# A decoder block on one core: convolution taps shared with ScalarE, attention dealt over weight tiles, merge products with tokens on the partition

## The chip, the cores and the metric

The kernel runs on one core of one Trainium2 chip. The metric is device time in microseconds (us) of one execution; the time before is 1765.85 us, the median of three runs (1764.63 to 1767.06). The engines are named as the profile names them: PE (TensorE matmul), PEld (its weight load), DVE (VectorE), ACT (ScalarE), POOL (GpSimd) and SP (SyncE, which issues most transfers).

## What is computed

One layer of a hybrid decoder for 256 tokens of width 2048, batch 1, all in float32:

```python
ada = silu(c) @ w_ada + b_ada                       # six vectors of 2048: shift, scale, gate, twice
h = rmsnorm(x) * (1 + sc1) + sh1
proj = h @ w_in                                      # 11824 columns: q, 6 x K/V, branch gates, GLU, merge gates
o_nsa = nsa_attention(q, k/v compressed, selected, window, gates)   # 16 heads of 128, 2 groups
y_a = o_nsa @ w_o_nsa
u = causal_dwconv(a * sigmoid(g), w_dw, b_dw)        # 31 taps per channel
y_b = silu(layernorm(u)) @ conv_pw_w + conv_pw_b
merged = sigmoid(ga) * y_a + sigmoid(gb) * y_b
x = x + g1 * (merged @ w_out)
h = rmsnorm(x) * (1 + sc2) + sh2
x = x + g2 * conv_ffn(h)                             # 2048 -> 2 x 5632 -> 2048
out = rmsnorm(x)
```

With 256 tokens every block is selected, and the window covers all earlier tokens, so that the selected and the window branch are two causal attentions over all keys.

## The kernel before

All weights, about 400 MB, are read once. A weight tile is 128 rows by 1024 numbers (for a product 512 columns wide: two of its sixteen blocks of 128 rows). `wtile` loads it into `raw` through SP's queue, ACT casts it to a rounded part `hi` (L213), and DVE subtracts to get the rest, `lo` (L214). Activations are split alike. A product is three matmuls per block, hi by hi, hi by lo and lo by hi, summed in PSUM. `raw` has four buffers; `hi` and `lo` have three in the pool `wp`, and between `more.__enter__()` (L467) and `more.__exit__` (L735) each fourth tile uses one more buffer out of a pool of its own.

There are three forms of product. `prod_x` (L228) has the activations as stationary operand and 512 weight columns moving; its result has tokens on the partition. `prod_w` (L240) has 128 weight columns as stationary operand and the 256 tokens moving; its result has channels on the partition. `prod_p` (L254) serves the up-projection of the last stage. Two result buffers of PSUM (`acc`) are shared by all of them.

The products follow each other: GLU columns (channel blocks 0 to 6 with the adaLN sums, then blocks 7 to 15), K/V, four chunks of queries (`q_chunk`), three of the four merge gates `gate_a`, four products with `w_o_nsa` (the fourth gate ahead of the last), four gates `C_MB`, four products with `conv_pw_w`, five with `w_out`, then the channel-mixing part. A `w_o_nsa` product takes the heads in their order: its tile number i needs heads 2i and 2i+1.

Other work is cut into steps in three queues: `heads_q` (attention), `conv_q` (convolution and its LayerNorm), `ada_q` (adaLN sums on DVE, each step a transfer of 512 KB into one of two `araw` buffers and one instruction, L280). After each weight tile `tick` (L117) gives out steps as long as the planned load of their engines is not above PE's. `drain` gives out what is left of a queue. The order on each engine is then set by a scheduler that models the time of each instruction; steps of `heads_q` get a higher priority. On the chip each engine runs its list in that order.

A step `scores(h)` makes the scores of one head for both branches, adds the distances (L684), takes the maximum (L686) and the exponential (L688); `values(h)` scales the rows (L704), transposes them (L709 to L711), copies them out of PSUM (L713), multiplies with the values (L714, L715) and splits the result into `oT`, the operand of the `w_o_nsa` products. `compressed(g)` does the compressed branch of a group of eight heads.

The convolution takes two channel blocks at a time (`conv_blocks`, L443): ACT makes the first product with the bias (L450), DVE adds 30 taps per block in place, one instruction of 128 by some 240 each (L457), and ACT copies the sum back (L460). The LayerNorm follows in steps once all blocks are done.

The merge keeps channels on the partition: `merged` gets `y_a` times its gate (L831), `gbs` the other gates (L840), and after each `conv_pw_w` product four instructions add the bias and multiply (L851), two add (L853) and the sums are split into `mT` (L854), the stationary operand of the `w_out` products.

## Time and profile before

| | |
|---|---|
| median of three runs | 1765.85 us |
| the profiled execution | 1765.94 us |
| its span, first to last instruction | 1764.2 us |
| PE busy | 1712.7 us, 97% |
| PEld busy | 1551.8 us, 88% |
| DVE busy | 1286.4 us, 73% |
| ACT busy | 872.9 us, 49% |
| mean granted PE clock | 0.986 of full speed |
| transfers | 402.8 MB read, 230 GB/s over the span |

Matmuls are pipelined and their ends are modelled, so that a busy PE need not run at its best rate; how fast it runs is seen from the distance between the starts of matmuls that follow each other. From 178 us on the products of the list above follow without a break: the second GLU products start there, the first `q_chunk` at 363, the first `gate_a` at 489, the first `w_o_nsa` product at 596, the first `C_MB` gate at 714, the first `conv_pw_w` product at 812, `w_out` at 907 and the channel-mixing part at 1012 us.

### The profile page before, as it was taken

How to read it: one execution, taken by the hardware profiler on the slowest of the kernel's cores; microseconds unless marked ns; L12 is line 12 of the kernel's file. 1: busy time of each engine (PE TensorE's matmuls, PEld its weight loads, DVE VectorE, ACT ScalarE, POOL GpSimd, SP SyncE). 2: the span in 40 equal slices, each digit the busy share in tenths (PEclk: the TensorE clock that was granted, in tenths of full speed). 3: DMA queues.
4: the chain of work that ended last, by engine and by line, in shares of the span. 5: the costliest groups of instructions: out<-in, count | busy, mean ns of one | idle time of the engine just before them, and what ended most of it. 6: DMA issues, size and time to landing. Idle time of an engine off the chain costs nothing.

```text
span 1764.2 us, 29690 instructions
## 1 busy us (share of the span) xinstructions
PE 1712.7 (97%) x11844; PEld 1551.8 (88%) x11844; DVE 1286.4 (73%) x1852; ACT 872.9 (49%) x1223; POOL 5.5 (0%) x22
## 2 busy tenths in 40 slices
PE   5999999999999999999999899999999999999997
PEld 3777999899999999999988888888888888888886
DVE  2233999998999898877886677776467776586665
ACT  4333444344768634563344465554455554345553
POOL 0000000000000000000000000000000000000000
PEclk8999999999999999999999999999999999999999
DMA  9996777884764676789887667676666767656663
GB/s 305 352 345 225 228 225 231 266 286 143 235 198 130 203 241 214 250 300 317 292 306 259 199 202 226 215 224 222 219 213 212 220 213 219 212 183 189 188 192 127
DMA packets 270198, 406.83 MB, mean 231 GB/s; under 512 B 12876, under 2 KB 181612, under 8 KB 269420
## 3 DMA queue, kind: packets, MB, share of 16 engines
q1 hardware_dynamic: 268652, 400.49, 71.4%
q10 hardware_dynamic: 1408, 4.46, 0.7%
q8 instruction: 92, 1.51, 0.4%
q14 instruction: 46, 0.38, 0.1%
HBM read 402.80 MB, written 2.10 MB: 230 GB/s over the span
## 4 chain that ended last, share of the span: by engine, by line
PE 93%; DMA 3%; DVE 2%; ACT 1%; issue 1%; SPq 0%; DVEq 0%; ACTq 0%
PE accp L261 18%; PE accw L251 11%; PE accw L248 11%; PE accw L250 11%; PE accp L262 9%; PE accx L236 6%; PE accx L237 6%; PE accx L235 6%; DMA araw<-in_w_ada_dram 2%; PE pt L379 1%; PE pt L675 1%; DVE lo L214 1%; PE pt L714 1%; PE pt L409 1%; PE pt L410 1%; PE pt L411 1%
## 5 line engine op out<-in xcount | busy, mean ns | idle before, releaser
L213 ACT CAST hi<-raw 128x1024 fp32r<-128x1024 f32 (+2 forms) x562 | 575.1, 1024 | 765.9 <-PE accw L250 273.3
L214 DVE TENSOR_TENSOR lo<-raw,hi 128x1024 fp32r<-128x1024 f32 (+2 forms) x562 | 668.6, 1191 | 375.4 <-ACT hi L213 363.8
L261 PE MATMUL accp<-act,hi 128*128 128x512 f32 x1408 | 492.4, 395 | 0.0
L251 PE MATMUL accw<-act,lo 128*128 128x256 f32 x1696 | 484.1, 286 | 2.0 <-DVE lo L214 2.0
L250 PE MATMUL accw<-act,hi 128*128 128x256 f32 x1696 | 483.8, 285 | 0.0
L248 PE MATMUL accw<-act,hi 128*128 128x256 f32 x1696 | 483.8, 285 | 0.0
L262 PE MATMUL accp<-act,lo 128*128 128x256 f32 x1408 | 393.6, 280 | 0.0
L251 PEld LDWEIGHTS accw<-act,lo 128*128 128x128 f32 x1696 | 325.5, 192 | 5.0 <-DVE lo L214 3.0
L248 PEld LDWEIGHTS accw<-act,hi 128*128 128x128 f32 x1696 | 325.8, 192 | 3.2 <-issue 2.4
L250 PEld LDWEIGHTS accw<-act,hi 128*128 128x128 f32 x1696 | 325.7, 192 | 2.4 <-issue 2.2
L261 PEld LDWEIGHTS accp<-act,hi 128*128 128x128 f32 x1408 | 264.1, 188 | 62.1 <-issue 0.2
L262 PEld LDWEIGHTS accp<-act,lo 128*128 128x128 f32 x1408 | 265.6, 189 | 0.3 <-issue 0.2
L236 PE MATMUL accx<-lo,act 128*128 128x512 f32 (+2 forms) x664 | 227.6, 343 | 1.3 <-DVE lo L214 1.3
L235 PE MATMUL accx<-hi,act 128*128 128x512 f32 (+2 forms) x664 | 227.2, 342 | 0.0
L237 PE MATMUL accx<-hi,act 128*128 128x512 f32 (+2 forms) x664 | 226.8, 342 | 0.0
L457 DVE SCALAR_TENSOR_TENSOR cacc<-big,cw,cacc 128x255 f32<-128x255 f32 (+24 forms) x480 | 201.3, 464 | 0.3
L280 DVE SCALAR_TENSOR_TENSOR t<-araw,cs,t 128x1024 f32<-128x1024 f32 x120 | 153.6, 1280 | 25.3 <-DMA araw<-in_w_ada_dram 25.2
L236 PEld LDWEIGHTS accx<-lo,act 128*128 128x128 f32 x664 | 125.8, 189 | 18.4 <-DVE lo L214 2.6
L235 PEld LDWEIGHTS accx<-hi,act 128*128 128x128 f32 x664 | 125.8, 189 | 14.5 <-ACT hi L213 0.2
L237 PEld LDWEIGHTS accx<-hi,act 128*128 128x128 f32 x664 | 125.8, 189 | 14.3 <-issue 0.4
L918 DVE SCALAR_TENSOR_TENSOR t<-t,fw,t 128x254 f32<-128x254 f32 (+1 forms) x176 | 73.5, 478 | 0.0
L916 ACT ACTIVATE t<-t,fw 128x256 f32<-128x256 f32 x88 | 48.0, 593 | 1.3 <-DVE t L913 1.3
(214 smaller groups left out, 1198.7 us busy)
## 6 DMA issues: line engine op xcount, KB each, us to landing
araw<-in_w_ada_dram SPq DMA_DIRECT2D x192, 512.0 KB, 5.4
raw<-in_ffn_w_up_dram SPq DMA_DIRECT2D x176, 512.0 KB, 4.5
raw<-in_w_in_dram SPq DMA_DIRECT2D x116, 512.0 KB, 4.6
raw<-in_ffn_w_down_dram SPq DMA_DIRECT2D x88, 512.0 KB, 4.7
raw<-in_w_in_dram SPq DMA_DIRECT2D x48, 384.0 KB, 3.9
raw<-in_w_o_nsa_dram SPq DMA_DIRECT2D x32, 512.0 KB, 4.7
raw<-in_conv_pw_w_dram SPq DMA_DIRECT2D x32, 512.0 KB, 5.5
raw<-in_w_out_dram SPq DMA_DIRECT2D x32, 512.0 KB, 4.7
```

The lines of the kernel that those rows point to most:

```text
L213: nc.scalar.copy(hi[:, :n], raw[:, :n])
L214: los.append(nc.vector.tensor_tensor(lo[:, :n], raw[:, :n], hi[:, :n], op=ALU.subtract).ins)
L235: nc.tensor.matmul(o, act[:, k, 0, s], hi, start=k == 0, stop=False)
L236: nc.tensor.matmul(o, act[:, k, 0, s], lo, start=False, stop=False)
L237: nc.tensor.matmul(o, act[:, k, 1, s], hi, start=False, stop=k == nk - 1)
L248: nc.tensor.matmul(acc[:, b, :], hi[:, s], act[:, k, 0, :], start=k == 0 and b % 2 == 0, stop=False, skip_group_check=True)
L250: nc.tensor.matmul(acc[:, b, :], hi[:, s], act[:, k, 1, :], start=False, stop=False, skip_group_check=True)
L251: nc.tensor.matmul(acc[:, b, :], lo[:, s], act[:, k, 0, :], start=False, stop=last, skip_group_check=True)
L261: nc.tensor.matmul(acc[:, b], hi[:, s], act[:, k], start=k == 0, stop=False, skip_group_check=True)
L262: nc.tensor.matmul(acc[:, b, 0, :], lo[:, s], act[:, k, 0, :], start=False, stop=k == KB - 1, skip_group_check=True)
L280: nc.vector.scalar_tensor_tensor(acc, raw, cs[:, k:k + 1], acc, op0=ALU.mult, op1=ALU.add)
L457: nc.vector.scalar_tensor_tensor(acc[:, s:], u[:, b, :T - s], cw[:, CW - 1 - s, b:b + 1], acc[:, s:], op0=ALU.mult, op1=ALU.add)
```

## The change

The convolution takes three blocks at a time into one wide tile `cacc`. For 18 of the 31 taps (`WIDE`) ACT makes three products, one per block, into `cprod`, and DVE adds all three with one instruction of 128 by some 720 (`wide`); 12 taps stay as they were, and the first product too. `cacc` and `cprod` have one buffer each; the last addition writes back to `u`, so that the copy L460 goes. The pool with the extra `hi` and `lo` buffers goes.

Steps of `heads_q` are no longer given out by planned load but at an even rate per weight tile, which `deal(n)` sets: the steps then in the queue over n tiles. `AHEAD` falls from 2 to 1: scores run one head ahead of values, and the score tiles have two buffers in place of three. `PACE`, the planned cost of the transfer of an adaLN step, rises from 5000 to 6500, and planned PE time from 2.53 to 2.75 per column. The adaLN steps for `g1` enter their queue when the convolution and the LayerNorm steps queued by then have been given out (`conv_done`) and not at the end of the attention.

Sixteen products (four each of `gate_a`, `w_o_nsa`, `C_MB`, `conv_pw_w`) go from `prod_w` to `prod_x`. The merge has tokens on the partition, with the bias loaded as a row for all partitions; `merged` is turned back by 32 transposes on PE (`turn_m`), given out three and four tiles after their product through the list `coming`.

```diff
-AHEAD = 2
+AHEAD = 1
-PACE = 5000
+PACE = 6500
...
+    def deal(n):
+        share[:] = len(heads_q) / n, 0.0
...
     def tick():
+        for c in coming:
+            c[0] -= 1
+        while coming and coming[0][0] <= 0:
+            coming.popleft()[1]()
+        share[1] += share[0]
+        while heads_q and share[1] >= 1.0:
+            share[1] -= 1.0
+            give(heads_q)
...
-            for q in queues:
+            for q in (conv_q, ada_q):
...
-        pool, bufs = (ext[0], 1) if ext[0] is not None and turn[0] % 4 == 0 else (wp, 3)
-        hi = pool.tile([P, WT], F32R, tag="hi", name=nm("hi"), bufs=bufs)
-        lo = pool.tile([P, WT], F32R, tag="lo", name=nm("lo"), bufs=bufs)
+        hi = wp.tile([P, WT], F32R, tag="hi", name=nm("hi"))
+        lo = wp.tile([P, WT], F32R, tag="lo", name=nm("lo"))
...
+    WIDE = tuple(s for s in range(2, CW) if s % 5 not in (0, 2)) + (1,)
...
+        def product(b, s):
+            def f():
+                if b == b0:
+                    box["p"] = cvp.tile([P, n, T], F32, tag="cprod", name=nm("cprod"))
...
+                nc.scalar.mul(box["p"][:, b - b0, s:], u[:, b, :T - s], cw[:, CW - 1 - s, b:b + 1])
+            return f
+
+        def wide(s):
+            def f():
+                acc, prod = box["a"], box["p"]
+                if s == 1:
+                    nc.vector.tensor_add(u[:, b0:b0 + n, :], acc, prod)
+                else:
+                    nc.vector.tensor_add(acc[:, :, s:], acc[:, :, s:], prod[:, :, s:])
+            return f
...
+        narrow = deque(({"dve": 470}, tap(b, s)) for s in range(2, CW) if s not in WIDE for b in blk)
+        for s in WIDE:
+            conv_q.extend(({"act": 500}, product(b, s)) for b in blk)
+            conv_q.extend(narrow.popleft() for _ in range(min(n, len(narrow))))
+            conv_q.append(({"dve": 170 + n * 265}, wide(s)))
...
-        gp = prod_w(h1, w_in, C_MA + n * 512, 512)
-        sg = sgt([P, 4, T])
+        gp = prod_x(h1, w_in, C_MA + n * 512, 512)
+        sg = sgt([P, NT, 512])
...
         heads_q.extend(compressed(0) + heads(0, HG))
+        deal(18)
         q_chunk(2)
         q_chunk(3)
         heads_q.extend(compressed(1) + heads(HG, HG))
+        deal(23)
         sga = [gate_a(n) for n in range(3)]
...
-        yp = prod_w(oT, w_o_nsa, n * 512, 512)
-        nc.vector.tensor_mul(merged[:, 4 * n:4 * n + 4, :], yp, sg)
+        yp = prod_x(oT, w_o_nsa, n * 512, 512)
+        nc.vector.tensor_mul(merged[:, :, n * 512:(n + 1) * 512], yp, sg)
...
+    def turn_m(b):
+
+        def f():
+            p_ = pt([P, 2, T])
+            for j in range(2):
+                for t in range(NT):
+                    nc.tensor.transpose(p_[:, j, t * P:(t + 1) * P], merged[:, t, (b + j) * P:(b + j + 1) * P], ident)
+            split(mT[:, b:b + 2], p_)
...
+        yp = prod_x(uT, conv_pw_w, n * 512, 512)
+        y = t4([P, NT, 512])
+        for t in range(NT):
+            nc.vector.tensor_add(y[:, t, :], yp[:, t, :], bias)
+            nc.vector.tensor_mul(y[:, t, :], y[:, t, :], gbs[:, t, s])
+            nc.vector.tensor_add(merged[:, t, s], merged[:, t, s], y[:, t, :])
+        coming.extend([3 + i, turn_m(4 * n + 2 * i)] for i in range(2))
```

Three places show how the order on the engines moves. The first is PE where the second group of eight heads meets the first `w_o_nsa` product. Before, that product (written accw, with `act` as the operand `oT`) has started while transposes (L709 to L711) and value products (L714, L715) of late heads of the group stand between its matmuls:

```order
L251 MATMUL accw_6514<-act_189,lo_6753 128x256
L248 MATMUL accw_6794<-act_4536,hi_6796 128x256
...
L248 MATMUL accw_6794<-act_4536,hi_6796 128x256
L709 MATMUL pt_6175<-ident,s_6036 128x128
L714 MATMUL pt_6144<-t_884_6150,big_3234 128x256
L710 MATMUL pt_6175<-ident,s_6041 128x128
L715 MATMUL pt_6144<-t_884_6150,big_3234 128x128
```

Now, in the same place, the first four of that product's eight tiles stand ahead, and behind them the group begins: the transposes of the compressed part (L699), the scores of its first heads (L718) and their values (L749 to L758), with no matmul of a product between.

```order
L250 MATMUL accx_6727<-hi_6800,act_4680 128x512
L699 MATMUL pt_5930<-ident,t_865_5909 128x128 x4
L718 MATMUL pt_5965<-big_3302,big_4008 128x2x128
L718 MATMUL pt_5967<-big_3302,big_4008 128x512
...
L749 MATMUL pt_6055<-big_3302 128x256
L752 MATMUL pt_6057<-ident,s_5971 128x128
...
L753 MATMUL pt_6160<-ident,s_6019 128x128
...
L248 MATMUL accx_6727<-hi_6825,act_4680 128x512
```

All eight heads of the second group have moved behind the first half of the first `w_o_nsa` product, into its second half and the product after it.

The second place is ACT in the middle of a group of heads. Before, what stands between the exponentials (L688), scalings (L704) and copies (L713) of the heads are casts of weight tiles (L213) and a few instructions of the convolution:

```order
L688 ACTIVATE s_5756,st_5750<-s_5756,st_5749 128x256 x2
L713 COPY t_809_5805<-pt_5801 128x384
L704 ACTIVATE s_5697<-s_5697,st_5708 128x128 x2
L704 ACTIVATE s_5702<-s_5702,st_5708 128x256 x2
L713 COPY t_811_5813<-pt_5809 128x384
L213 CAST hi_6550<-raw_6549 128x1024
L460 COPY big_190<-cacc_5452 128x256
L460 COPY big_190<-cacc_5454 128x256
L213 CAST hi_6583<-raw_6582 128x1024
```

Now, at the start of the second group, products of the last three convolution blocks (L495) stand between the exponentials (L731) and scalings (L747), three for each tap:

```order
L226 CAST hi_6874<-raw_6873 128x1024
L701 COPY big_3302<-pt_5930 128x512
L495 ACTIVATE cprod_6469<-big_190,cw 128x245 x3
L731 ACT_TABLE_LOAD
L731 ACTIVATE s_5971,st_5970<-s_5971,st_5969 128x128 x2
L731 ACTIVATE s_5976,st_5970<-s_5976,st_5969 128x256 x2
L495 ACTIVATE cprod_6560<-big_190,cw 128x243 x3
L731 ACTIVATE s_6014,st_6013<-s_6014,st_6012 128x128 x2
L731 ACTIVATE s_6019,st_6013<-s_6019,st_6012 128x256 x2
L747 ACTIVATE s_5971<-s_5971,st_5982 128x128 x2
L747 ACTIVATE s_5976<-s_5976,st_5982 128x256 x2
L495 ACTIVATE cprod_6661<-big_190,cw 128x242 x3
```

From the copy L701 to the last head's split stand 39 such products, eight heads and seven casts of weight tiles on ACT.

The third place is PE in the fourth `conv_pw_w` product. Before, only its matmuls stand there; now the transposes of the columns that the third one finished (L903) are set among them, a first one early and three later, for two pairs of blocks:

```order
L248 MATMUL accx_8868<-hi_8940,act_7681 128x512
L903 MATMUL pt_8929<-ident,big_6725 128x128
L903 MATMUL pt_8957<-ident,big_6725 128x128
L249 MATMUL accx_8868<-lo_8941,act_7681 128x512
...
L248 MATMUL accx_8868<-hi_8971,act_7681 128x512
L903 MATMUL pt_8929<-ident,big_6725 128x128 x3
L903 MATMUL pt_8957<-ident,big_6725 128x128 x3
L249 MATMUL accx_8868<-lo_8972,act_7681 128x512
```

The turned columns of the last product stand in the same way inside the first `w_out` product.

## Rows read from the trace of the kernel before

**Rows 1.** The page: busy time of engines; the chain that ended last, by engine.

```profile
PE 1712.7 (97%) x11844; PEld 1551.8 (88%) x11844; DVE 1286.4 (73%) x1852; ACT 872.9 (49%) x1223; POOL 5.5 (0%) x22
...
PE 93%; DMA 3%; DVE 2%; ACT 1%; issue 1%; SPq 0%; DVEq 0%; ACTq 0%
```

**Rows 2.** PE in order of time: start us, duration, instruction; inside a prod_w product.

```profile
459.14 0.28 PE L248 MATMUL accw<-act,hi 128*128 128x256 f32 x1
459.26 0.28 PE L250 MATMUL accw<-act,hi 128*128 128x256 f32 x1
```

**Rows 3.** The same, inside a prod_x product 512 columns wide.

```profile
960.18 0.39 PE L237 MATMUL accx<-hi,act 128*128 128x512 f32 x1
960.41 0.39 PE L235 MATMUL accx<-hi,act 128*128 128x512 f32 x1
960.64 0.39 PE L236 MATMUL accx<-lo,act 128*128 128x512 f32 x1
```

**Rows 4.** Stretches: length, busy (instructions) by engine, PE clock, DMA; one product each.

```profile
789.30:812.30 23.00, 23.00 (x194) 23.00 (x193) 16.49 (x14) 9.30 (x9) 0.00 (x0) 1.00 0.92 304
...
957.70:979.40 21.70, 21.70 (x97) 18.00 (x96) 12.20 (x12) 9.78 (x12) 0.00 (x0) 1.00 0.69 221
```

**Rows 5.** PE in order of time: two transposes that follow each other.

```profile
463.22 0.27 PE L709 MATMUL pt<-ident,s 128*128 128x128 f32 x1
463.33 0.27 PE L710 MATMUL pt<-ident,s 128*128 128x128 f32 x1
```

**Rows 6.** Stretches with attention, all instructions.

```profile
413.60:595.60 182.00, 182.00 (x1340) 171.22 (x1339) 165.35 (x361) 124.67 (x294) 0.52 (x1) 0.98 0.55 165
595.60:624.30 28.70, 28.70 (x233) 28.18 (x232) 25.06 (x39) 15.37 (x23) 0.00 (x0) 1.00 0.82 274
```

**Rows 7.** The first of them, only what writes or reads the tile accw.

```profile
413.60:595.60 182.00, 133.38 (x962) 121.57 (x961) 0.00 (x0) 5.07 (x5) 0.98 0.55 165
```

**Rows 8.** Groups by line: busy us, mean ns, idle before; ACT's work for the heads.

```profile
L688 ACT ACTIVATE s<-s,st 128x128 f32<-128x128 f32 (+1 forms) x64 | 28.5, 447 | 1.4 <-DVE st L686 1.1
...
L704 ACT ACTIVATE s<-s,st 128x128 f32<-128x128 f32 (+1 forms) x64 | 23.8, 446 | 1.1 <-DVE st L694 1.1
...
L713 ACT COPY t<-pt 128x384 f32<-128x384 f32 x32 | 14.6, 473 | 9.1 <-PE pt L711 8.9
...
L688 ACT ACTIVATION_READ_ACCUMULATOR s<-s,st 128x1 f32 x64 | 12.1, 189 | 0.0
...
L329 ACT CAST act<-pt 128x256 fp32r<-128x256 f32 x16 | 5.9, 370 | 12.5 <-PE pt L715 12.4
```

**Rows 9.** Groups by line and shape, ACT: casts of weights, a scaling, a first product.

```profile
L213 ACT CAST hi<-raw 128x1024 fp32r<-128x1024 f32 x476 | 499.9, 1051 | 639.2 <-PE accw L250 225.8 <-PE accx L237 169.3 <-PE accp L261 154.8
...
L704 ACT ACTIVATE s<-s,st 128x256 f32<-128x256 f32 x32 | 14.3, 497 | 0.0
...
L450 ACT ACTIVATE cacc<-big,par,cw 128x256 f32<-128x256 f32 x16 | 9.3, 598 | 0.5 <-DVE big L436 0.4
```

**Rows 10.** Groups by line, DVE: taps, and a product of 128 by 768.

```profile
L457 DVE SCALAR_TENSOR_TENSOR cacc<-big,cw,cacc 128x255 f32<-128x255 f32 (+24 forms) x480 | 201.3, 464 | 0.3
...
L480 DVE TENSOR_TENSOR big<-accw,sg 128x768 f32<-128x768 f32 x3 | 2.9, 950 | 0.0
```

**Rows 11.** Stretches: GLU to second query chunk; a C_MB gate; two w_out products; their end.

```profile
177.90:413.60 235.70, 235.70 (x1983) 227.28 (x1982) 219.08 (x386) 102.57 (x127) 1.27 (x3) 1.00 0.81 245
...
737.70:766.30 28.60, 27.69 (x221) 26.53 (x220) 25.50 (x26) 24.01 (x32) 0.00 (x0) 1.00 0.75 249
...
907.40:957.70 50.30, 48.96 (x233) 40.26 (x232) 37.10 (x40) 21.56 (x25) 0.00 (x0) 1.00 0.85 286
...
1002.00:1012.30 10.30, 5.76 (x31) 5.47 (x29) 8.63 (x31) 6.07 (x15) 0.00 (x0) 0.70 0.80 262
```

**Rows 12.** The chain that ended last, 895 to 935 us: start us, us, what.

```profile
898.92 5.54 DMA araw<-in_w_ada_dram
...
905.86 5.42 DMA araw<-in_w_ada_dram
...
924.79 6.82 DMA araw<-in_w_ada_dram
```

144 lines of the change are left out of this document (73 added, 71 removed).

## The prediction

> **What bounds the kernel now.** I read first the page's busy shares and its chain. PE is busy 97% of the span, and 93% of the chain that ended last is PE [rows 1]: the time is the length of PE's stream plus the gaps in which something comes late. So an edit is priced by what it adds to or takes from that stream, and work on DVE, ACT or a queue costs only where PE then waits for it. Since a busy PE need not run at its best rate, I next read PE in order of time for the distance between starts [rows 2, 3, 5], and then stretches cut at the first matmul of each product, in which a product's own length stands beside what it took here [rows 4, 6, 7, 11]. The groups by line give the durations on ACT and DVE [rows 8 to 10]. The sum is made against the profiled execution, 1765.9 us (a span of 1764.2 and 1.7 around it), which is 0.1 above the median of the runs, so a result by it stands for the median too.
>
> **Sixteen products in another form.** A `prod_w` matmul of 256 columns starts 0.12 us after the one before it (459.14, 459.26) [rows 2]; a product has 192 of them, 23.0 us, and an undisturbed one took 23.00 [rows 4]. A `prod_x` matmul of 512 columns starts 0.23 us after its predecessor (960.18, 960.41, 960.64) [rows 3]; a product has 96, and an undisturbed one took 21.70 with 97 [rows 4]. So one wide matmul costs some 13 ns less than two narrow ones, 1.25 us per product (my value, between the 1.3 of the stretches and the 1.2 of the rounded starts), and the sixteen products get 20.0 us shorter. This term rests on a form that before uses already for `w_out`.
> The Trainium skill speaks against it: "TensorE: Matmul & The Clock Gate", section Back-to-back issue gap, gives as the isolated gap of warm matmuls the columns divided by 2.4 plus 2.5 ns, so that joining two saves 2.5 ns; for 1536 joined pairs that is an estimate of 3.8 us in place of 20. The trace does not agree: 0.12 and 0.23 us stand above the page's 0.109 and 0.216. The same section gives 131 ns for 512 columns in a stream of weight loads and matmuls, which no row here comes near.
>
> **The merge.** The `turn_m` steps add 32 transposes; two that follow each other start 0.11 us apart (463.22, 463.33) [rows 5], so 3.5 us; if none overlapped, 32 x 0.27 = 8.6. I take 3.5, since they stand in a stream of matmuls. They are given out three and four tiles after their product, and the last ones are needed by `w_out` only at tile 6 of 8, 16 us after that product began; DVE's merge (four instructions per 512 columns, and now six of 128x512 and a split) has that long: nothing on the path. The sigmoids are as many numbers as before.
>
> **Attention.** Before, 182 us with two query chunks and three gates hold 962 matmuls of accw [rows 6, 7], 962 x 0.12 = 115.4. The other 66.6 us, and the 28.7 - 23.0 = 5.7 by which the first `w_o_nsa` product is longer [rows 6], are 72.3 us for 16 heads and the compressed parts: 4.5 us of PE per head, waits included. ACT needs per head (28.5 + 12.1 + 23.8 + 14.6 + 5.9) / 16 = 5.3 us [rows 8].
> The first group now lies over two chunks and three gates: 2 x 23 + 3 x 21.8 = 111, with 8 x 4.5 = 36 makes 147 us of PE. ACT has there 8 x 5.3 = 42.5, some 40 casts at 1.051 [rows 9], some 81 products at 0.497 (a scaling of 128x256 [rows 9]) and copies of 6 us: 131. It fits, and with half the heads in that stretch some of the old waits go: -3 (between -6 and 0).
> The second group is not even. By the order it lies behind four tiles of the first `w_o_nsa` product, with 39 convolution products between its steps. From the copy L701 on ACT has 39 x 0.497 = 19.4, 8 x 5.3 = 42.5, seven casts 7.4 and some 2 for the copy and a table: 71 us. PE has 36 and ten tiles of 21.7 / 8 = 2.7: 63. PE cannot run ahead, since its next matmuls read what ACT's steps make: +8 at least. `cprod` and `cacc` have one buffer, so that in each of 13 steps ACT can wait for DVE's addition, about 0.95 us by the product of 128x768 [rows 10]: 0 to 13 more. I take +9, near the lower end, because the order puts exponentials and scalings between the products, which fill the time of an addition. Both groups: +6, from +2 to +21.
>
> **Convolution.** From the GLU to the second chunk DVE is busy 219.1 of 235.7 us and ACT 102.6, and PE loses little [rows 11]. Before, 242 of the 480 taps lie there at 201.3 / 480 = 0.42 [rows 10]: 101 us. Now, by the order, 108 taps (45 us), 40 additions of up to 768 columns (0.93, somewhat under the 0.95 of [rows 10]: 37) and 18 of one block (0.4: 7): 89. DVE gains 12 us in the stretch that it bounds next. ACT gets some 150 products at 0.497 (between 0.45 and the 0.598 of a first product [rows 8, 9]): 75 more, 178 of 234 us. What can be lost is the slack: the fourth `hi` and `lo` are gone, and DVE now waits for ACT's products, ahead of splits on its queue that PE needs. +1, from -1 to +6.
>
> **LayerNorm and adaLN steps.** The second `C_MB` product took 28.6 us for 23 [rows 11], beside the LayerNorm. The convolution now ends inside the second `w_o_nsa` product and the LayerNorm moves with it: 0, from -4 to +3. Two `w_out` products took 50.3 us [rows 11] for 2 x 21.7 and 1.8 of waiting work, some 5 lost while the chain waits for `araw` transfers of 5.4 to 6.8 us [rows 12]. By the order none of these steps stands in `w_out` now; 25 stand in the four `conv_pw_w` products, 31 in the five before. They read as many bytes, one transfer of 512 KB each beside a weight stream that already moves 304 GB/s [rows 4], so the loss may come back there. +1.5, from -8 to +8 with what a full queue of SP costs the weight tiles behind it.
>
> **Clock.** In the stretch of attention the granted clock was 0.98 on average [rows 6], and 0.70 around PE's wait for the adaLN sums at 1002 to 1012 [rows 11], that is, part of the time at the lower level of 1.2 GHz. 0.02 x 182 = 3.6 us is what the first one cost. A longer wait in the second group could bring one such stretch more: 0 in the sum, up to +7 in the range.
>
> **Sum.** 1765.9 - 20.0 + 3.5 + 6 + 1 + 0 + 1.5 = 1757.9, so 1758 us. What lies before 178 and after 1012 us stays.
>
> **The rivals.**
> A, cover everywhere: the attention costs +2, the waits of `w_out` and LayerNorm go (-5 and -3 in place of +1.5 and 0): 1757.9 - 4 - 6.5 - 3 = 1744, at 1741 to 1751. For it: no `araw` step in `w_out`, and the LayerNorm is spread. Against it: ACT's 71 us against PE's 63.
> E, the gain is half given back: attention at +12 with the `cprod` waits, or the convolution at +6: 1762 to 1769, near no change.
> B, ACT becomes the bound, and the result is slower: in the second group the `cprod` turns cost their full 13 us, attention is +21 less nothing from the first group, the clock falls once more (+3.6): 1765.9 - 20 + 3.5 + 21 + 3.6 + 1 + 1.5 = 1776.6, at 1770 to 1778. It decides once all losses together pass 16.5 + 3.5 = 20 us. For it: the order shows no product's matmul between the transposes and values of the second group, so nothing fills PE's waits. Against it: its scores run one head ahead.
> C, the change does not shorten PE's stream: if the columns alone set the distance of starts, a wide matmul takes 2 x 0.12 = 0.24 us, the first term is 0 and the sum 1777.9; with some of A's cover 1772 to 1778. The rows stand against it [rows 2 to 4], which show both forms at a granted clock of 1.00.
> By the Trainium skill's section Back-to-back issue gap (its 3.8 us in place of 20.0) the time would be an estimate of 1774, inside C.
> That the steps are not dealt evenly, as the change says, is seen in the order already and is in the sum.
>
> **Chances and range.** The forecast, 1752 to 1762, has 0.38; A 0.22, E 0.17, B 0.20, C 0.03. The likeliest gives the time, 1758. The range of 8 in 10 goes from 1743, which leaves out the lower end of A, to 1776, which takes in C and most of B: 1743 to 1776. A measurement of this kernel tells some 0.2% from no change, 3.5 us. Faster than 1762.3 are the forecast and A, 0.60; E lies within, 0.17; B and C are slower, 0.23.
>
> **What the profile after will show.** Starts of accx 0.23 us apart in gates and `conv_pw_w`, and undisturbed products of 21.7 us, show the first term right; 0.24 would make it wrong. The transposes of `turn_m` should start 0.11 us apart with no wait ahead. The first two `w_o_nsa` products should take together about 43.4 + 36 + 9 = 88 us with ACT busy nearly throughout and PE idle in front of transposes and values; 80 or less speaks for A, 100 and a granted clock under 1.00 for B. From 178 to 413 PE should lose no more than now, with DVE less busy and ACT near three quarters. `w_out` should have products of 21.7, and the `conv_pw_w` ones at most 2 us more than that each; if the chain waits for `araw` or for weight tiles there by more, the +1.5 is wrong. What would make the whole wrong is a place that I do not see in these rows: weight tiles late in the stretch of attention for want of the fourth buffer, or a cast behind a product that waits for DVE.

## The result: 1.5% slower

The changed kernel takes 1792.6 us (median of four runs, 1788.1 to 1795.0) against 1765.2 of the kernel before in the same comparison: a ratio of 1.0147, with a 95% interval of 1.0125 to 1.0170. The forecast was 1758 with a range of 1743 to 1776: wrong in its sign, and outside the range. The profiled execution, the longest of the four, took 1794.96 us, 29.0 more than that of before.

### The profile page after: what moved, and what is told of

Read it like the earlier page. It is cut to its first block, busy times and chain, and to the rows that moved or that the text cites. A ratio compares the mean times of both kernels' runs of the same rounds, so it can differ in the third digit from the quotient of the medians.

```text
span 1793.0 us, 26879 instructions
## 1 busy us (share of the span) xinstructions
PE 1711.8 (95%) x10340; PEld 1475.5 (82%) x10340; DVE 1266.2 (71%) x1672; ACT 981.5 (55%) x1497; POOL 6.1 (0%) x28
## 4 chain that ended last, share of the span: by engine, by line
PE 84%; DVE 6%; DMA 5%; ACT 3%; issue 2%; DVEq 0%; SPq 0%; ACTq 0%
PE accp L281 18%; PE accx L249 11%; PE accx L248 11%; PE accx L250 11%; PE accp L282 9%; PE accw L263 4%; PE accw L262 4%; PE accw L260 4%; DMA araw<-in_w_ada_dram 4%; DVE lo L227 2%; PE pt L399 1%; DVE t L300 1%; PE pt L718 1%; PE pt L429 1%; PE pt L430 1%
## 5 line engine op out<-in xcount | busy, mean ns | idle before, releaser
L249 PE MATMUL accx<-lo,act 128*128 128x512 f32 (+2 forms) x1176 | 434.0, 369 | 14.5 <-DVE lo L227 14.4
L248 PE MATMUL accx<-hi,act 128*128 128x512 f32 (+2 forms) x1176 | 429.8, 366 | 4.4 <-ACT hi L226 2.2
L250 PE MATMUL accx<-hi,act 128*128 128x512 f32 (+2 forms) x1176 | 430.1, 366 | 0.0
L249 PEld LDWEIGHTS accx<-lo,act 128*128 128x128 f32 x1176 | 223.1, 190 | 55.3 <-DVE lo L227 20.3
L248 PEld LDWEIGHTS accx<-hi,act 128*128 128x128 f32 x1176 | 222.9, 190 | 40.9 <-ACT hi L226 2.7
L250 PEld LDWEIGHTS accx<-hi,act 128*128 128x128 f32 x1176 | 223.3, 190 | 35.4 <-issue 2.3
L263 PE MATMUL accw<-act,lo 128*128 128x256 f32 x672 | 191.4, 286 | 0.4 <-DVE lo L227 0.4
L260 PE MATMUL accw<-act,hi 128*128 128x256 f32 x672 | 190.7, 284 | 0.0
L262 PE MATMUL accw<-act,hi 128*128 128x256 f32 x672 | 190.5, 284 | 0.0
L495 ACT ACTIVATE cprod<-big,cw 128x248 f32<-128x248 f32 (+17 forms) x288 | 123.7, 488 | 19.5 <-DVE cacc L504 17.5
L260 PEld LDWEIGHTS accw<-act,hi 128*128 128x128 f32 x672 | 128.8, 192 | 2.0 <-issue 2.0
L263 PEld LDWEIGHTS accw<-act,lo 128*128 128x128 f32 x672 | 128.6, 192 | 2.3 <-issue 1.7
L262 PEld LDWEIGHTS accw<-act,hi 128*128 128x128 f32 x672 | 128.8, 192 | 1.9 <-issue 1.9
L504 DVE TENSOR_TENSOR cacc<-cacc,cprod 128x756 f32<-128x756 f32 (+25 forms) x102 | 83.8, 822 | 8.3 <-ACT cprod L495 5.3
```

Source lines behind the costliest of these rows:

```text
L248: nc.tensor.matmul(o, act[:, k, 0, s], hi, start=k == 0, stop=False)
L249: nc.tensor.matmul(o, act[:, k, 0, s], lo, start=False, stop=False)
L250: nc.tensor.matmul(o, act[:, k, 1, s], hi, start=False, stop=k == nk - 1)
L260: nc.tensor.matmul(acc[:, b, :], hi[:, s], act[:, k, 0, :], start=begin and k == first and b % 2 == 0, stop=False, skip_group_check=True)
L262: nc.tensor.matmul(acc[:, b, :], hi[:, s], act[:, k, 1, :], start=False, stop=False, skip_group_check=True)
L263: nc.tensor.matmul(acc[:, b, :], lo[:, s], act[:, k, 0, :], start=False, stop=last, skip_group_check=True)
```

## The profile after

First the page: busy time of engines, and the chain that ended last by engine.

```profile
PE 1711.8 (95%) x10340; PEld 1475.5 (82%) x10340; DVE 1266.2 (71%) x1672; ACT 981.5 (55%) x1497; POOL 6.1 (0%) x28
...
PE 84%; DVE 6%; DMA 5%; ACT 3%; issue 2%; DVEq 0%; SPq 0%; ACTq 0%
```

PE was 93% of the chain before [rows 1] and is 84% now, DVE, ACT and transfers 14% where they were 6%: PE waits for them more. Now PE in order of time, in an undisturbed product of the new form (start us, duration, instruction), and a set of the added transposes:

```profile
823.89 0.39 PE L248 MATMUL accx<-hi,act 128*128 128x512 f32 x1
824.12 0.39 PE L249 MATMUL accx<-lo,act 128*128 128x512 f32 x1
824.35 0.39 PE L250 MATMUL accx<-hi,act 128*128 128x512 f32 x1
...
923.45 0.82 PE L903 MATMUL pt<-ident,big 128*128 128x128 f32 x6
```

The starts are 0.23 us apart as in [rows 3], and six transposes take 0.82, that is 0.11 each and the length of the last: the prices of a product and of a transpose were right. The Trainium skill ("TensorE: Matmul & The Clock Gate", section Back-to-back issue gap) gives 2.5 ns above the columns' time for each isolated matmul; the trace does not agree here either: eighteen distances from 901.75 to 905.83 us are 0.227 each for 512 columns, against its 0.216.

Then stretches, cut at the first matmul of a product (length; busy us and instructions of PE, PEld, DVE, ACT and POOL; granted clock as a share of 2.4 GHz; DMA share; GB/s). The first line is from the third query chunk to the start of `w_o_nsa`; then the first two `w_o_nsa` products; the fourth; the second `C_MB` product; the fourth, undisturbed; the four with `conv_pw_w`; and two with `w_out`.

```profile
413.50:565.20 151.70, 151.70 (x910) 133.07 (x909) 136.58 (x231) 125.95 (x268) 0.72 (x3) 0.99 0.64 200
565.20:659.70 94.50, 79.34 (x365) 61.17 (x363) 73.67 (x142) 73.06 (x189) 0.10 (x1) 0.93 0.32 107
...
705.60:740.90 35.30, 29.11 (x112) 21.60 (x111) 28.24 (x27) 22.95 (x30) 0.00 (x0) 0.95 0.85 294
...
764.00:792.90 28.90, 23.65 (x98) 19.15 (x97) 16.92 (x15) 10.62 (x10) 0.00 (x0) 0.94 0.96 338
816.40:838.20 21.80, 21.80 (x98) 18.04 (x97) 12.00 (x10) 9.36 (x9) 0.00 (x0) 1.00 0.78 267
838.20:936.60 98.40, 95.22 (x441) 77.68 (x440) 81.96 (x84) 37.53 (x39) 0.00 (x0) 1.00 0.90 309
936.60:981.10 44.50, 44.50 (x201) 36.77 (x201) 26.82 (x28) 20.66 (x24) 0.00 (x0) 1.00 0.59 196
```

Two `w_o_nsa` products took 94.5 us where 2 x 21.75 is the products' own time; `w_out` came down from the 50.3 of [rows 11] to 44.5. To see all stretches against both forms of product, the table takes from each stretch 23.0 us for every `prod_w` and 21.75 for every `prod_x` in it. What is left is the work of heads and transposes on PE, and PE's waits. A stretch is cut where its first matmul starts, so that two to four microseconds may move to its neighbour (the -2.1 is such a case). Four columns are of experiments told below: e1 is the kernel before with the merge products alone; e15 the changed kernel with two convolution blocks at a time; e12 that with scores two heads ahead; e13 that with the planner's numbers of before.

| left over, us | before | after | e1 | e15 | e12 | e13 |
|---|---|---|---|---|---|---|
| third query chunk to second `w_o_nsa` | 72.7 | 91.5 | 82.1 | 84.3 | 77.5 | 79.0 |
| third and fourth `w_o_nsa`, last gate | -2.1 | 16.0 | -2.1 | 6.2 | 5.0 | 0.2 |
| four `C_MB` | 6.1 | 10.3 | 13.2 | 14.7 | 17.7 | 9.2 |
| four `conv_pw_w` (3.5 are transposes, not before) | 3.1 | 11.4 | 6.8 | 13.8 | 6.1 | 3.8 |
| two `w_out` | 6.8 | 1.0 | 10.1 | 0.9 | 3.1 | 7.7 |
| sum | 86.6 | 130.2 | 110.1 | 119.9 | 109.4 | 99.9 |

From before to after the sum grows by 43.6. The sixteen products give back 20.0, and what follows 1035 us is 5.9 longer (the last section): 29.5, of the 29.0 measured. 3.5 of the 43.6 are the transposes' own time; the rest was lost beside products that took what they were to take. Three places make most of it.

**The second group of heads.** PE and then ACT, in order of time (the idle time before an instruction, and what ended it, in brackets):

```profile
580.12 0.59 PE L749 MATMUL pt<-big 128*128 128x256 f32 x2
590.72 0.76 PE L752 MATMUL pt<-ident,s 128*128 128x128 f32 x2 [10.00 <-ACT s L747]
```

```profile
581.77 1.28 ACT L495 ACTIVATE cprod<-big,cw 128x245 f32<-128x245 f32 x3 [2.49 <-DVE cacc L504]
583.07 1.28 ACT L731 ACT_TABLE_LOAD   x1
584.37 0.40 ACT L731 ACTIVATE s<-s,st 128x128 f32<-128x128 f32 x1
...
587.35 1.27 ACT L495 ACTIVATE cprod<-big,cw 128x243 f32<-128x243 f32 x3 [1.12 <-DVE st L736]
588.53 0.39 ACT L731 ACTIVATE s<-s,st 128x128 f32<-128x128 f32 x1
...
590.28 1.47 ACT L747 ACTIVATE s<-s,st 128x128 f32<-128x128 f32 x4
```

PE has made the scores of two heads and waits 10 us for the scaled rows of the first: ACT waits 2.5 us for an addition of the convolution, makes three products, loads a table, takes the exponentials of the first head, makes three products, takes those of the second, and only then scales the first. The granted clock around it, in stretches:

```profile
576.00:583.30 7.30, 3.97 (x16) 2.07 (x14) 7.30 (x13) 4.21 (x9) 0.00 (x0) 1.00 0.59 199
583.30:597.00 13.70, 6.28 (x17) 4.13 (x18) 11.02 (x28) 12.57 (x41) 0.00 (x0) 0.50 0.03 12
597.00:604.00 7.00, 6.78 (x38) 5.35 (x37) 6.50 (x17) 6.99 (x23) 0.00 (x0) 1.00 0.01 2
```

In the wait the clock falls to half, 1.2 GHz, and stays there until 597.0: what PE does from 590.7 on costs twice: two transposes take 0.76 us there, and 0.38 at 919.91 where the granted clock is 1.00.

**The LayerNorm** stands now in the fourth `w_o_nsa` product (705.6 to 740.9, 35.3 us). ACT there, and PE's waits:

```profile
709.51 1.01 ACT L774 COPY sg<-accx 128x1024 f32<-128x1024 f32 x1
710.53 1.28 ACT L858 ACT_TABLE_LOAD   x1
711.83 4.05 ACT L858 ACTIVATE big<-big,par 128x256 f32<-128x256 f32 x8
715.90 1.28 ACT L880 ACT_TABLE_LOAD   x1
717.19 1.06 ACT L880 ACTIVATE sg<-sg 128x1024 f32<-128x1024 f32 x1
718.16 1.03 ACT L226 CAST hi<-raw 128x1024 fp32r<-128x1024 f32 x1
719.21 1.28 ACT L858 ACT_TABLE_LOAD   x1
720.50 3.06 ACT L858 ACTIVATE big<-big,par 128x256 f32<-128x256 f32 x6
...
724.46 2.92 ACT L226 CAST hi<-raw 128x1024 fp32r<-128x1024 f32 x3
```

```profile
714.19 0.50 PE L249 MATMUL accx<-lo,act 128*128 128x512 f32 x1 [2.62 <-DVE lo L227]
...
725.54 0.51 PE L248 MATMUL accx<-hi,act 128*128 128x512 f32 x1 [2.24 <-ACT hi L226]
```

The first of these waits comes from DVE. The weight tile was cast by 709.6, and its split stands behind the LayerNorm's four scalings:

```profile
708.37 4.62 DVE L852 TENSOR_TENSOR big<-big,t 128x1024 f32<-128x1024 f32 x4
712.92 1.22 DVE L227 TENSOR_TENSOR lo<-raw,hi 128x1024 fp32r<-128x1024 f32 x1
```

The second comes from ACT. Between 709.5 and 724.5 it casts one weight tile; the rest are a copy of the gate, silu, the gate's sigmoid and three table loads of 1.28 us to go from one to the other and back. PE uses up the `hi` tiles that are ready and waits; at 726.7 its clock falls to half for 3.4 us. (The Trainium skill, "ScalarE: Activation LUTs", section What ACT_TABLE_LOAD costs, gives 1.28 us for a load and 1.38 more for a drain with each switch. The trace agrees with the first and shows no drain: the copy before ends at 710.52, the load begins at 710.53, and the first silu at 711.83.)

**The adaLN steps** on DVE, in the second `C_MB` product:

```profile
767.68 1.22 DVE L227 TENSOR_TENSOR lo<-raw,hi 128x1024 fp32r<-128x1024 f32 x1
775.32 1.28 DVE L300 SCALAR_TENSOR_TENSOR t<-araw,cs,t 128x1024 f32<-128x1024 f32 x1 [6.42 <-DMA araw<-in_w_ada_dram]
776.52 3.49 DVE L227 TENSOR_TENSOR lo<-raw,hi 128x1024 fp32r<-128x1024 f32 x3
```

DVE stands 6.4 us before one adaLN transfer, with three splits of weight tiles queued behind it, while the transfers move 338 GB/s in this stretch. PE waits for the first of the three.

## Experiments

Each kernel is timed against the kernel before on the same chip, whose median was 1766.1 to 1768.0 in these comparisons; where two kernels of different comparisons are set against each other, this is part of the noise.

**The merge products alone.** The kernel before, with only this part of the change:

```diff
-        gp = prod_w(h1, w_in, C_MA + n * 512, 512)
+        gp = prod_x(h1, w_in, C_MA + n * 512, 512)
...
-        yp = prod_w(uT, conv_pw_w, n * 512, 512)
+        yp = prod_x(uT, conv_pw_w, n * 512, 512)
...
+        coming.extend([3 + i, turn_m(4 * n + 2 * i)] for i in range(2))
```

> The kernel before with one part of the change alone: the sixteen merge products in the prod_x form, the merge with tokens on the partition and the 32 transposes; convolution, attention and planner as before. If the product term of the sum was right (-20.0 for the products, +3.5 for the transposes) and lies on the path wherever it stands: 1749 us. If a gain in PE's stream is eaten because other engines then come late: 1757 to 1765. If the columns alone set the distance of starts: 1769.

1771.0 us, ratio 1.0030 (1.0014 to 1.0046): not faster, but slower. The undisturbed products do take 21.8, so it isn't the distance of starts, though the time is near the third figure. PE's waits for weight tiles from 413 to 1036 us show where part of the 20 us went, first before, then e1 (what waited, for whom: us in total, times, longest):

```profile
...
PE accw L251 <- DVE lo L214: 2.0, 3, 0.9
PE accx L236 <- DVE lo L214: 1.3, 3, 0.5
```

```profile
PE accx L242 <- DVE lo L220: 11.4, 14, 1.8
...
PE accx L241 <- ACT hi L219: 2.7, 1, 2.7
```

Waits for splits rise from 3.3 us to 11.4, and for casts from nothing to 2.7. DVE's work in the stretch of the attention is unchanged, 212.3 us busy of 233.7 before and 210.8 of 236.8 here:

```profile
413.60:647.30 233.70, 233.70 (x1762) 222.40 (x1761) 212.32 (x432) 150.10 (x327) 0.52 (x1) 0.99 0.60 187
```

```profile
415.20:652.00 236.80, 231.91 (x1283) 197.51 (x1282) 210.75 (x429) 150.20 (x328) 0.52 (x1) 0.98 0.58 183
```

The products got shorter, the stretch didn't: by the table 9.4 us of the 20 went there, 7.1 into `C_MB` and 3.3 into `w_out`.

**Lighter adaLN steps on e1, and on the kernel before.** To see whether other work holds PE up once its products are shorter, fifteen of sixteen steps are cut to a quarter, transfer and sum (e9a), or the sum alone (e9b); e9c is e9b's edit on the kernel before.

```diff
-                nc.sync.dma_start(raw, w_ada[k * P:(k + 1) * P, c0:c0 + WT])
+                w = WT if k == 0 else 256
+                nc.sync.dma_start(raw[:, :w], w_ada[k * P:(k + 1) * P, c0:c0 + w])
...
-                    nc.vector.scalar_tensor_tensor(acc, raw, cs[:, k:k + 1], acc, op0=ALU.mult, op1=ALU.add)
+                    nc.vector.scalar_tensor_tensor(acc[:, :w], raw[:, :w], cs[:, k:k + 1], acc[:, :w], ...)
```

> The kernel of e1_merge_only (before, with the merge products alone in the new form) with lighter adaLN steps: of each step but the first of sixteen, only the first 256 of 1024 columns are loaded and summed, the rest is left out of the computation; the planner's costs are unchanged. Theory SLACK (the 22 us by which e1_merge_only missed 1749 are adaLN transfers and sums that DVE waits for, with splits of weight tiles behind them): 1743 to 1752, the conv_pw_w and C_MB products at 22 to 23 us each. Rival: the merge's own work on DVE or the heads cost it; 1762 or more.

> As e9a_light_ada, but the transfers are whole and only the sums on DVE are short (256 of 1024 columns, the rest left out of the computation). If it is the wait for the transfer in DVE's queue: no better than 1763 to 1771. If it is DVE's work: as e9a_light_ada, below 1755.

> The kernel before with the short adaLN sums of e9b_light_sums (256 of 1024 columns, the rest left out of the computation). Theory SLACK (before has just enough of DVE, so that relief brings little there, and the shorter products use it up): 1761 to 1766, a gain of 5 at most, against 12 on e1_merge_only. Rival (relief of DVE is worth the same in both): 1751 to 1756.

1755.3, 1759.3 and 1770.2 us. On e1 the short sums are worth 11.7 and the short transfers 4.0 more; on the kernel before the same short sums are worth nothing (1.0016, 1.0002 to 1.0030), less even than SLACK had it. That is the interaction that the forecast left out: before had as much slack on DVE as it needed, and relief brought nothing; with shorter products the same sums cost time. e9b landed between its two figures, and e9a above its own, 6 us short of 1749: the attention's stretch is still 3 us longer than its products and heads of before would make it, and the LayerNorm still costs in `C_MB`, whose products took 25.6 each and not 22 to 23.

Where in the kernel DVE comes late is less clear than these totals. In the profiled execution of e9b the attention's stretch is no shorter than in e1, with 16 us less for DVE to do there; `w_out` is what got shorter, 46.3 us for two products in place of 53.6. And e11, told below, has the same 26 adaLN sums and some 182 taps in this stretch as e1, with DVE as busy, and takes 228.9 us: 74.2 left over by the table's measure, where e1 has 82.1 and before 72.7. (What e11 loses, it loses later: 11.0 are left over in `w_out`.) e9b, then e11:

```profile
415.40:653.90 238.50, 234.44 (x1283) 200.81 (x1282) 194.37 (x428) 150.71 (x328) 0.52 (x1) 0.96 0.57 183
413.10:642.00 228.90, 228.65 (x1282) 197.26 (x1281) 210.94 (x428) 150.69 (x328) 0.53 (x1) 0.99 0.61 191
```

So a busy share of nine tenths on DVE does not by itself eat the gain. What differs is when its steps come: the last ten of the 26 sums run from 613 to 652 us in e1, from 595 to 647 before and from 577 to 642 in e11, and four of e1's five waits for splits in this stretch lie between 625 and 644. That the crowding is the cause fits, but no run moves these steps alone.

**The convolution of before in the changed kernel.**

```diff
-    for b, n in ((0, 3), (3, 3), (6, 1)):
-        conv_blocks(b, n)
+    for b in range(0, NA - 1, 2):
+        conv_blocks((b, b + 1))
...
-        conv_blocks(b, 3)
+        while done + 2 <= b + 3:
+            conv_blocks((done, done + 1))
+            done += 2
```

> The changed kernel with the convolution of before (two blocks at a time, all 30 taps on DVE, the copy back on ACT); attention, merge and planner as changed. Theory ACT: the convolution products on ACT push the second group of heads, and behind it the LayerNorm, late; without them the stall of 10 us ahead of that group goes, and the time is 1760 to 1772. Rival DEAL: the even dealing with scores one head ahead makes the stall by itself; the time stays at 1785 or above. A granted clock under 0.95 in the second group's stretch would go with DEAL.

1780.8 us, 11.8 less than the changed kernel, between the two figures. The first two `w_o_nsa` products still took 88 us, although ACT made no products at all, PE still waited 4.8 us for the first scaled rows, and the granted clock over the two was 0.94, which was to go with DEAL. So ACT's products are not the whole of that stall, and the next run says whether they are any of it.

**Two blocks at a time, one head ahead.** The changed kernel, its 18 products on ACT kept, with only two blocks in one `cacc` and `cprod` (and the taps of the channel mixing loaded later, for the room that the run behind it needs).

```diff
-    for b, n in ((0, 3), (3, 3), (6, 1)):
-        conv_blocks(b, n)
+    for b in range(0, NA - 1, 2):
+        conv_blocks(b, 2)
...
-    fw = const.tile([P, 4, 2 * FB], F32, name="fw")
...
+        gate1["fw"] = late.tile([P, 4, 2 * FB], F32, name="fw", tag="fw")
```

> The kernel of e12_wide2_ahead (1768.1) with AHEAD back at 1: against the changed kernel (1792.6) it differs only in the convolution of two blocks at a time and the later load of the channel mixing's taps. Theory CHAIN (the depth of the scores is what cost): 1782 to 1792. Rival (three blocks in one pair of tiles are what cost, since ACT and DVE hand them over in longer pieces): 1766 to 1774.

1780.3 us: between the two figures, and the same as e2 without the products. So with two blocks ACT's products cost nothing on balance; going from two blocks to three in one pair of tiles cost 12, unless the later load of the taps, which was not run alone, has a part in it. The 12 us divide by the table into 7 in the attention (the wait of 10.0 is 4.8 here) and 10 around the fourth `w_o_nsa` product, since the LayerNorm came out elsewhere, less 7 given back in `C_MB` and `conv_pw_w`. Why three blocks came out so much worse than two isn't shown: ACT's waits for DVE's additions are alike, 17.5 us and 18.4 in all. The longer pieces ahead of a head's scalings, as in the ACT rows above, fit, but are only argued.

**Two heads ahead.** e6 is e2 with `AHEAD` at 2, e12 is e15 with it, e10 the changed kernel with it and a raw buffer less; e5 is the kernel before with one ahead.

```diff
-AHEAD = 1
+AHEAD = 2
...
-        raw = wp.tile([P, WT], F32, tag="raw", name=nm("raw"), bufs=4)
+        raw = wp.tile([P, WT], F32, tag="raw", name=nm("raw"), bufs=3)
```

(The second piece in e10 alone; in e5 the first one the other way round.)

> The kernel of e2_conv_before (the changed kernel with the convolution of before) with AHEAD at 2, for which its attention has room. Against 1780.75 of that: theory CHAIN: 1768 to 1774, and the first two w_o_nsa products fall from 88 us to about 78. Theory LOAD: 1778 to 1784, and they stay at 85 or more.

> The changed kernel with AHEAD at 2 and all four raw buffers; the room comes from a convolution of two blocks at a time in place of three (18 taps still as products on ACT) and from loading the taps of the channel mixing later. Theory CHAIN: 1774 to 1782 (the changed kernel less 10 to 18). Theory LOAD (ACT's products hold the heads up whatever the depth): 1786 or more.

> The changed kernel, its convolution products on ACT included, with AHEAD at 2; the room for it comes from one of the four buffers for raw weight tiles. Theory CHAIN (with scores two ahead the softmax of a head is ready when PE comes to it, as e6_two_ahead against e2_conv_before: -15): 1774 to 1782, and the first two w_o_nsa products at 85 us or less, from 94. Theory LOAD (in the changed kernel ACT's products stand in front): 1787 or more. The lost buffer can cost some us by itself.

> The kernel before with AHEAD at 1 alone (scores one head ahead, two buffers of score tiles). Theory CHAIN (each head's softmax is waited for once scores run only one head ahead, and the heads fall back behind the weight tiles): 1772 to 1780, with the first two w_o_nsa products at 60 us or more together, where they took 51.7. Theory LOAD (what the engines have to do sets it, not the depth): 1763 to 1769.

e6: 1766.0 us, 14.7 less than e2. e12: 1768.1, 12.2 less than e15. Both went the way of theory CHAIN and came out below its range. In both the wait for scaled rows is gone; PE's waits from 413 to 1036 us in after, and in e12 (the longest ones):

```profile
PE accx L249 <- DVE lo L227: 14.4, 12, 5.2
PE pt L752 <- ACT s L747: 10.0, 1, 10.0
...
PE accx L248 <- ACT hi L226: 2.2, 1, 2.2
```

```profile
PE accx L248 <- DVE lo L226: 10.1, 10, 2.7
...
PE accx L247 <- ACT hi L225: 2.4, 1, 2.4
```

e10 keeps three blocks: 1790.2, by its time a failure of the theory. Its stretches say more. The first two `w_o_nsa` products took 83.9 in place of 94.5, and no wait for scaled rows is left; but with three raw buffers the third query chunk began 8.4 us later than in the changed kernel (421.9), and the fourth `w_o_nsa` product took 38.5. The lost buffer ate most of the gain. e5: on the kernel before one head ahead costs 2.7 us (1.0017, 1.0000 to 1.0035), not the 6 and more that theory CHAIN wanted. CHAIN's other figure did come true: the first two `w_o_nsa` products took 74.9 us in place of 51.7. But they began 19.6 us earlier, and from the third query chunk to their end it is 236.9 against 233.7. So heads that move into these products lengthen them without being lost; the whole stretch is what counts. The depth is worth 12 to 15 us where the heads come late and bunched, and hardly anything where they don't.

**The planner's numbers.**

```diff
-PACE = 6500
+PACE = 5000
...
-        use(dma=1.43 * n, act=190 + n / 1.2, dve=150 + n / 0.96)
+        use(dma=1.43 * n, act=190 + n / 1.2, dve=60 + n / 0.96)
...
-            use(pe=m * w * 2.75)
+            use(pe=m * w * 2.53)
```

(All three in e4, the last alone in e14. The middle one, the planned time of a split on DVE, is a part of the change too. The price of 1500 that the change sets for the adaLN steps of `g1` stays in both.)

> The changed kernel with the planner's numbers of before: 2.53 in place of 2.75 per column of PE, 5000 in place of 6500 for an adaLN transfer, 60 in place of 150 for a split. Theory ACT: 2.53 gives out fewer convolution steps per weight tile, so the convolution ends later and the LayerNorm with it; no better than 1788. Rival PLAN: 2.75 fills DVE and ACT to the brim, and the waits in front of casts and splits come from that: 1770 to 1780.

> The changed kernel with one number of the planner as before, 2.53 per column of PE in place of 2.75; the others stay. Theory: the 16 of e4_plan_before come from fewer steps per weight tile, so that the LayerNorm leaves the w_o_nsa products: 1774 to 1781. Rival: they come from the adaLN transfers' price: 1786 or more.

1776.0 and 1778.0 us: the 2.53 alone brings 14.6 of the 16.5. A `prod_x` column takes 21.75 us / 8192 = 2.65 ns, so at 2.75 the planner gives out more steps per weight tile than PE's time covers; at 2.53 fewer. In both runs the third and fourth `w_o_nsa` products and the last gate have 0.6 left over in place of 16.0, since the LayerNorm leaves them; the second group still bunches (e14: 64 us in the first `w_o_nsa` product alone).

**The LayerNorm later.** Its steps enter their queue behind the four `w_o_nsa` products.

```diff
-    conv_q.extend(({"dve": d, "act": a}, f) for d, a, f in
...
     merged = bigt([P, NT, D])
     for n in range(4):
...
+    conv_q.extend(({"dve": d, "act": a}, f) for d, a, f in
```

> The changed kernel with one thing moved: the LayerNorm steps enter their queue behind the four w_o_nsa products, so that they run beside the C_MB gates as before. Theory PLACE (the 13 us that the fourth w_o_nsa product lost come from where the LayerNorm stands, beside gates, copies and sigmoids on ACT): that product falls from 35 to 24 us at most, a C_MB product takes 6 more, and the time is 1784 to 1788. Rival: the LayerNorm costs the same wherever it stands, and the time stays within 1789 to 1796.

1786.5 us: 6.1 less (1.0085 to 1.0133 against 1.0125 to 1.0170, which overlap a little). The fourth product fell from 35.3 to 24.7, and the `C_MB` products took 101.3 in place of 97.3. So about half of the 13.5 us that the fourth product had lost seems to hang on the place; the other half goes with the steps.

**Almost no convolution.**

```diff
-    WIDE = tuple(s for s in range(2, CW) if s % 5 not in (0, 2)) + (1,)
+    WIDE = (1,)
...
-        narrow = deque(({"dve": 470}, tap(b, s)) for s in range(2, CW) if s not in WIDE for b in blk)
+        narrow = deque(({"dve": 470}, tap(b, s)) for s in range(2, 3) for b in blk)
```

> The changed kernel with only three of the 31 taps (two narrow ones and one as a product and addition); the other 28 are left out of the computation, so DVE and ACT lose nearly all of the convolution while attention, merge, LayerNorm and adaLN steps are as changed. Theory LOAD (the convolution's work stands in front of the heads on DVE and ACT and pushes the second group late): the first two w_o_nsa products take 60 us or less together, in place of 94, and the time is 1750 to 1762. Theory CHAIN (one head ahead, single buffers): 80 us or more, and 1770 to 1785. What is left above 1749 is what the LayerNorm and the adaLN steps cost with no convolution.

1766.7 us. The first two `w_o_nsa` products took 59.3 us, as LOAD wanted, with one head ahead and the even dealing; so here, as in e5, one head ahead costs little. The total missed its figure by 4.7. The products ran as shown, and still the time was that of before: by the table's measure 7.9 us are left over in the third and fourth `w_o_nsa` products, 9.0 in `C_MB` and 9.4 in `conv_pw_w`, so LayerNorm and adaLN steps cost there with almost no convolution.

**How the steps are given out.** By planned load again, in the changed kernel (e3) and in e13 (e16).

```diff
-        share[1] += share[0]
-        while heads_q and share[1] >= 1.0:
-            share[1] -= 1.0
-            give(heads_q)
...
-            for q in (conv_q, ada_q):
+            for q in (heads_q, conv_q, ada_q):
```

> The changed kernel with the attention steps given out by planned load again, ahead of convolution steps, as before (scores still one head ahead, since a third buffer of score tiles has no room). Theory ACT: the work on ACT is the same, so within 8 us of the changed kernel, 1785 to 1798. Rival DEAL: 1765 to 1778, with the second group spread over the gates.

> The kernel of e13_wide2_ahead_plan (1759.9) with attention steps given out by planned load, ahead of the others, in place of the even dealing. If the dealing costs by itself: 1752 to 1757. If depth and planner were all: 1757 to 1763. If even dealing is a gain: above 1764.

1786.4 and 1765.0 us: 6.2 less than the changed kernel, inside theory ACT's range and far from DEAL's, and 5.1 more than e13. So the even dealing probably costs a little with one head ahead and is probably a gain with two (the intervals, 1.0098 to 1.0131 and 1.0125 to 1.0170, 0.9945 to 0.9978 and 0.9971 to 0.9996, overlap a little).

**What is faster than both.** e13 is e12 with the planner's numbers of before; e11 is the same with the convolution of before, that is e6 with those numbers.

> The kernel of e6_two_ahead (changed kernel with the convolution of before and scores two ahead) with the planner's numbers of before as in e4_plan_before. If both effects are apart (-15 and -16 against their kernels): 1750 to 1757, which would beat the kernel before. If they take away the same waits: 1762 to 1768.

> The kernel of e12_wide2_ahead with the planner's numbers of before (2.53 per column, 5000 per adaLN transfer, 60 for a split). It differs from e11_two_ahead_plan (1759.6) in the convolution alone. If the products on ACT relieve DVE where DVE holds PE up: 1748 to 1757. If what they put on ACT costs the heads as much or more: 1759 to 1772.

1759.6 us (ratio 0.9965, 0.9952 to 0.9979) and 1759.9 (0.9962, 0.9945 to 0.9978). Both beat the kernel before, by 0.35 and 0.38%; e11 lies between its two figures, e13 in the range of its second theory. They differ in the convolution and in when the channel mixing's taps are loaded, and the products on ACT bring nothing there, with DVE 200.4 us busy in the attention's stretch against 210.9. The steps from the changed kernel to e13 are 12.3 (two blocks), 12.2 (two ahead) and 8.2 (planner), 32.7 in all; the planner's part was 16.5 on the changed kernel itself, so the three overlap.

## Why the prediction was wrong

Three terms failed: the gain of the products, entered in full; the attention, in which the step from two heads ahead to one had no price; and the LayerNorm, set at nothing.

- **What bounds the kernel.** "Work on DVE, ACT or a queue costs only where PE then waits for it" was right as a sentence, and the term built on it was not. A stream without breaks was read as PE being the bound alone. e1 shows that with products 1.25 us shorter PE waits for splits, 11.4 us in place of 3.3. DVE's load (212 of 234 us in the attention's stretch) is not shown to be the reason: e11 has the same load and loses 1.5 us there.
- **Sixteen products, -20.0.** The price per product was right, as the rows of after show (one of its two supports was not: the rounded starts give 1.0 per product, not 1.2). As a gain of time it failed: e1 alone gave +4 in place of -16.5. I made no allowance for cover lost elsewhere; weight tiles that come late were named as what would make the whole wrong, and given no price. e9b against e9c shows it for DVE's sums: worth 11.7 with the short products, nothing without. That the same products lose 1.5 us in the attention's stretch of e11 and 9.4 in that of e1 shows that the gain hangs on how the steps beside them are given out.
- **Transposes, +3.5.** Right; no wait ahead of them in the rows shown.
- **Attention, +6, from +2 to +21.** It came out at 18.8, near the upper end, and the reason given for the lower end was wrong. I said that B has the one-head depth against it; the depth was the weak point (-12 and -15 in e12 and e6), and I had not priced `AHEAD` going from 2 to 1 at all. The first two `w_o_nsa` products were forecast at 88 us and measured 94.5; the 13.7 us at half clock, some 6.9 of them lost, are about the difference, and the +9 left no room for it. ACT was to be busy nearly throughout and was so for 73.1 of the 94.5 us. The sum of ACT's work (71 us against 63) was beside the point: e2, without the products, and e15, with them, take the same time.
- **Convolution, +1.** From 178 to 413 us PE lost nothing, as forecast: 235.8 us there, 235.7 before, so that the fourth `hi` and `lo` buffers, which served this stretch alone, were not missed. DVE was busy 208.1 us there, as asked, ACT 160.6 in place of 178. The sum put no gain on the relief of DVE, and e11 against e13 shows none.
- **LayerNorm, 0, from -4 to +3.** It moved beside the last gate and cost 13.5 us in the product where it stands; the trace of before showed 5.6 for it in `C_MB` [rows 11], and I let "it moves" stand for "it costs nothing". The order showed what stands between casts on ACT, and ahead of splits on DVE, and I didn't read it.
- **adaLN steps, +1.5, from -8 to +8.** `w_out` got its 5.8 back as said. The same waits came back in `C_MB` (+4.2) and `conv_pw_w` (+8.3 less the transposes' 3.5). Net +3.2, inside the range, and in part by luck: the LayerNorm's 5.6 had left `C_MB`, and counted without it the adaLN steps cost 8.8. By the sign that the forecast gave, `conv_pw_w` products of at most 23.7 us, the term was wrong: they took 24.6.
- **Clock, 0 to +7.** From 178 to 1036 us the clock stood at half for 13.6 us before and 27.3 after, so some 6.8 us more are lost to it. It was in the range as an extra. 20.5 of the 27.3 begin in or right behind waits of PE (at 583.3, 726.7 and 777.9 us) and should have gone with them; the fall at 559.4 has no such wait ahead of it.
- **The rest stays.** The stages behind 1035 us took 5.9 us more in the profiled execution; see below.
- **Rivals.** B had the direction, for another reason: the one-head depth, three blocks in a pair of tiles and 2.75 per column, while ACT's products were no cause that the runs show. (Its sum is 1776.5, not 1776.6.) B's upper end of 1778 left out that the LayerNorm and the adaLN steps could go wrong together with the heads, since all of them are placed by the same planner. C is out by the starts 0.227 us apart.

## What stays open

Why the shorter products alone gain nothing (e1) is known by stretch and not by cause: the crowded steps of DVE fit, and were not moved by themselves. Why three blocks cost 12 us more than two is not settled, since depth, planner and blocks move the LayerNorm about, and part of each difference is where it happens to land. Two heads ahead with three blocks and all buffers was not tried, for want of room.

## To carry to other kernels

When one engine streams without a break, do not price a shorter stream in full before it is clear that the steps beside it still come in time: the same sixteen products gained nothing in e1, while in e11, with the same work for DVE given out at other times, the five in the attention's stretch gave most of their price (4.8 us of 6.25). Steps that fill in beside a stream are handed out against its planned speed, so a change of that speed, or of how far ahead a chain of dependent steps runs, is priced as a change of its own. And a step that moves takes its cost with it: read what now stands in front of the casts and splits at its new place.

## What the runs showed of the hardware

The up-projection's products, alike in work and instructions, run at two rates at a granted clock of 1.00. Ten of them in the kernel before, first one and then the other, and ten of after:

```profile
1058.10:1169.10 111.00, 111.00 (x643) 97.10 (x642) 84.01 (x107) 62.90 (x80) 0.00 (x0) 1.00 0.72 223
1292.60:1405.70 113.10, 113.10 (x643) 98.11 (x642) 83.41 (x106) 62.56 (x80) 0.00 (x0) 1.00 0.69 214
```

```profile
1070.20:1183.30 113.10, 113.10 (x642) 98.05 (x641) 85.76 (x109) 62.90 (x80) 0.00 (x0) 1.00 0.72 223
```

111.0 and 113.1 us for the same ten products. In the kernel before the first and third stage of the channel mixing run at the one rate and the second at the other. What comes after `w_out` took 751.9 us in the profile of before, 757.8 in that of after, and between 751.9 and 758.3 in those of the kernels whose work there is the same. What sets the rate stays open. It makes up to 6 us of a single profile's difference, so that stretches, not spans, were compared above; the spread of the kernel before over 25 runs, 1760.9 to 1772.1, is of that size.
